# Sixteen projection pairs of a hybrid decoder block as seven-product blocks in a stage of their own

## The chip, the core and the metric

The kernel runs on one core of one Trainium2 chip. The metric is the device time of one execution, in microseconds. Before the change three runs gave 1787.57, 1789.16 and 1790.8 us (median 1789.16). The engines are called as in the profile: PE (TensorE: matmuls and transposes; PEld is its weight load, which lies beside the matmuls), DVE (VectorE), ACT (ScalarE), POOL (GpSimd) and SP (SyncE, which here issues most DMA loads). Each engine runs its own instructions strictly in the order in which they stand in the program; semaphores tie the engines together.

## The reference, cut to what matters

One decoder layer on 1024 tokens of 1024 channels. `h` is projected by one wide matrix whose columns feed two mixers and two merge gates.

```python
h = rmsnorm(x, norm_mix)
proj = h @ w_in
(rq, rk, rv, rg,                          # retention: 4 heads, dk 128, dv 256
 nq, kcr, vcr, ksl, vsl, kwn, vwn, ngate, # sparse attention: 8 heads, dk 64, 2 KV groups
 ga, gb) = split(proj)                    # merge gates, 1024 columns each
y_a = retention(rq, rk, rv, rg, ret_gn_g) @ w_ret_o
# nsa: compressed blocks (kcr, vcr through a small MLP), the top 8 of 16 selected
# blocks (ksl, vsl), a window of 512 (kwn, vwn); three softmaxes, mixed by ngate
y_b = nsa(nq, kcr, vcr, ksl, vsl, kwn, vwn, ngate, ...) @ w_nsa_o
x = x + (sigmoid(ga) * y_a + sigmoid(gb) * y_b) @ w_out
x = x + conv_ffn(rmsnorm(x, norm_ffn), ...)
return rmsnorm(x, norm_final)
```

All is float32. The kernel reaches that precision with three passes per product: an operand is split into a high and a low part (`split`: a copy on ACT that rounds to the matmul's type, then a subtraction on DVE), and `mm3` adds high x high, high x low and low x high.

## The kernel before, in words

The transposed activations `hTh`, `hTl` (high and low part, two tiles of four channel blocks each) stay in SBUF from the first stage until retention ends. The stages follow one another in the program.

1. **Norm and values** (0 to 46 us of the profiled execution). For each of 8 token tiles: load, norm (`hx`), eight transposes on PE, two splits. `values(t)`, two tiles later, multiplies a tile with the 280 columns of the values and the branch gates.
2. **Compress** (46 to 140.6 us). `proj_T` projects 128 columns of `w_in` for all 1024 tokens: 2 halves x 8 channel blocks x 3 passes = 48 matmuls of 512 columns. Called for KC and VC (by `blocks`, which builds the overlapping blocks `xr` on DVE straight out of PSUM), for the four query pairs (`queries`, to the DRAM buffer `q_scr`) and for the keys KW and KS (`keys`, into the tiles `kst`). `hidden` and `compressed` are the small MLP; its matmuls wait for `xh` and `xl`, the split blocks.
3. **Attention** (140.6 to 649.7 us). 16 units: 8 query tiles from the last to the first, 2 KV groups each; the later units see fewer keys and are shorter. A unit is a long chain across engines: scores on PE (`ps_sc`), mask and maximum on DVE (`pw`, `psl`, `pc`), exponentials on ACT, scaling on DVE, transposes on PE (`ps_pt`), split into `pth` (ACT) and `ptl` (DVE), product with the values on PE (`ps_pv`), output `ot` on DVE. Between these stand projections that have nothing to do with attention, here called the fill: after each unit `stored` projects 128 columns of a merge gate (GA, then GB) and stores them to DRAM, after every fourth unit a `ret_block` projects one head's 256 columns of retention's gate (RG), and the values (RV) of two heads close the list. A `ret_block` has 8 token tiles x 8 channel blocks x 3 passes = 192 matmuls of 256 columns.
4. **Retention** (649.7 to 870 us). Four heads. Each head projects its q and k by `proj_T`; two heads read their values from DRAM (`v_raw`), two project them in the loop over chunks.
5. **Output projections, merge, FFN** (to the end). The FFN's up projection already uses `seven`: a 2 x 2 block product in seven products instead of eight, each of 4 channel blocks x 3 passes of 512 columns, with sums and differences of the blocks (`s1` to `s4` of the activations, `t1` to `t4` of the weights).

The order of instructions on each engine is fixed when the program is built, by a scheduler that moves independent work (the fill above all) ahead into places where it reckons PE free; program order is only its starting point.

Of the kernel before, what the change touches and what calls it, by code (L numbers as in the profile page):

```python
# [10 lines left out]
F32 = mybir.dt.float32  # L11
# [7 lines left out]
P = 128  # L19
# [21 lines left out]
SPILL_V = 2  # L41
SPILL_Q = 0
# [42 lines left out]
def tile_hybrid_block(ctx: ExitStack, tc: tile.TileContext, x, norm_mix, w_in, ret_gn_g,  # L85
# [8 lines left out]

    const = ctx.enter_context(tc.tile_pool(name="const", bufs=1))
# [19 lines left out]
    rv_scr = scratch("rv_scr", SPILL_V, (S, DV))  # L115
    rq_scr = scratch("rq_scr", SPILL_Q, (P, S))
# [15 lines left out]
    def mm3(ps, ah, al, bh, bl, start, stop, more=False):  # L132
        nc.tensor.matmul(ps, ah, bh, start=start, stop=False, skip_group_check=more)  # L133
        nc.tensor.matmul(ps, ah, bl, start=False, stop=False, skip_group_check=more)  # L134
        return nc.tensor.matmul(ps, al, bh, start=False, stop=stop, skip_group_check=more)  # L135

# [54 lines left out]

    with ExitStack() as st:
        pool = st.enter_context(tc.tile_pool(name="p0", bufs=2))
        gm = pool.tile([P, D], F32, name="gm", bufs=1)
        for t in range(NT):
            xt = pool.tile([P, D], F32, name="xt", bufs=4)
            x_load = nc.sync.dma_start(xt, x[t * P:(t + 1) * P, :])
            if t == 0:
                nc.sync.dma_start(gm, bcast(norm_mix[0], D))
            if t < 3:  # L200
                value_weights(*((0, 3), (3, 3), (6, 2))[t])
# [6 lines left out]
            tok = slice(t * P, (t + 1) * P)  # L208
            for i in range(2):
# [5 lines left out]
            if t >= 2:  # L215
                values(t - 2)
        values(NT - 2)
        values(NT - 1)

    def proj_T(c0, evac, wts=None):  # L220

        wh, wl = wts or weights([(w_in, c0, P)])
        for hf in range(2):
            ps = bank("mm")
            tok = slice(hf * 512, hf * 512 + 512)
            for k in range(KD):
                mm3(ps, wh[:, k, :], wl[:, k, :], hT[k][0][:, tok], hT[k][1][:, tok],
                    k == 0, k == KD - 1)
            evac(hf, ps)

# [5 lines left out]
    with tc.issue_after(x_load.ins):  # L236
        nc.sync.dma_start(tab, tab_nsa)
# [10 lines left out]
    def blocks(c0, pos):  # L248
        c2 = [cpool.tile([P, S], F32, name=f"c2{g}") for g in range(NG)]

        def evac(hf, ps):
            t0 = hf * 512
            for g in range(NG):
                src = ps[g * DK:(g + 1) * DK, :]
                nc.scalar.activation(c2[g][0:DK, t0:t0 + 512], src, AF.Copy)
                if hf == 0:
                    nc.vector.tensor_copy(c2[g][DK:P, 0:511], src[:, 1:512])
                else:
                    nc.vector.tensor_copy(c2[g][DK:P, 511:1023], src)

        proj_T(c0, evac)
# [78 lines left out]
    def queries(pr):  # L340
        def evac(hf, ps):
            qe = npool.tile([P, 512], F32, name="ge", bufs=2)
            nc.scalar.activation(qe, ps, AF.Copy, scale=tab[:, T_QS + pr:T_QS + pr + 1])
            nc.scalar.dma_start(
                q_scr[pr][:, :, hf * 512:hf * 512 + 512].rearrange("h d t -> (h d) t"),
                qe)
        proj_T(C_NQ + pr * P, evac)


    def keys(b, c0):  # L350
        def evac(hf, ps):
            k0, k1 = (k[:, 4 * hf:4 * hf + 4, 0:P] for k in kst[b])
            ps = ps.rearrange("p (t k) -> p t k", k=P)
            nc.scalar.activation(k0[0:DK], ps[0:DK], AF.Copy)
            nc.scalar.activation(k1[DK:P], ps[DK:P], AF.Copy)
            nc.vector.tensor_sub(k0[DK:P], ps[0:DK], f32(k0[0:DK]))
            nc.vector.tensor_sub(k1[0:DK], ps[DK:P], f32(k1[DK:P]))
        proj_T(c0, evac)

    xk = blocks(C_KC, cmp_pos_k)  # L360
    xv = blocks(C_VC, cmp_pos_v)
    queries(0)
    queries(1)
    hk = hidden(xk, cmp_w1_k, cmp_b1_k, cmp_w2_k)
    hv = hidden(xv, cmp_w1_v, cmp_b1_v, cmp_w2_v)
    queries(2)
    queries(3)
# [5 lines left out]
    keys(1, C_KW)  # L373
    keys(0, C_KS)
# [154 lines left out]
    def stored(scr, c0):  # L529

        def evac(hf, ps):
            ge = npool.tile([P, 512], F32, name="ge", bufs=2)
            nc.scalar.activation(ge, ps, AF.Copy)
            nc.scalar.dma_start(scr[:, hf * 512:hf * 512 + 512], ge)
        proj_T(c0, evac)

# [24 lines left out]
    for h in range(SPILL_Q):  # L561
        stored(rq_scr[h], C_RQ + h * P)
# [3 lines left out]
    with ExitStack() as st:  # L566
# [32 lines left out]
        for h in range(H_R):  # L599
# [198 lines left out]

# [281 lines left out]
```

## Time and profile before

| | before |
|---|---|
| runs, us | 1787.57, 1789.16, 1790.8 |
| profiled execution, us | 1790.46 |
| its span, us | 1788.7 |
| PE busy | 1740.3 us, 97% |
| DVE busy | 1074.4 us, 60% |
| ACT busy | 767.5 us, 43% |
| PE instructions | 9137 |

The span is the time between the first and the last instruction of the profiled execution; 1.76 us of its time lie around it. Busy time is the union of an engine's instructions. DVE's 60% is a mean over stages of quite different load, so the stages are to be read one by one. In the windows below, the columns after the engines are the granted clock of PE (1.00 is its full speed), the mean busy share of the DMA engines and the GB/s that they moved.

### The profile page before, as it was taken

To read this page: it belongs to the slowest core of one execution; us is meant where nothing else is said; L and a number is where in the kernel's file an instruction comes from. 1 tells how busy PE (TensorE), PEld (TensorE's weight loads), DVE (VectorE), ACT (ScalarE), POOL (GpSimd) and SP (SyncE) were. 2 spreads that over 40 slices of the span, in tenths; PEclk is the share of its full clock that TensorE was granted. 3 is DMA by queue.
4 is the path that set the end of the run, shared out by engine and by line. 5 is a ranking of instruction groups with operands and counts; after the bars stand their busy time and mean duration, and the time that the engine had idled before them with its cause. 6 is when DMAs were issued, how large, how long until landed. Compare 5 with 4: busy or idle time off the path is not lost.

```text
span 1788.7 us, 24018 instructions
## 1 busy us (share of the span) xinstructions
PE 1740.3 (97%) x9137; PEld 1481.9 (83%) x9137; DVE 1074.4 (60%) x2279; ACT 767.5 (43%) x1392; POOL 87.3 (5%) x94
## 2 busy tenths in 40 slices
PE   8999999999999999999999897999999999999998
PEld 7888898988989998899778786888888888788886
DVE  6537676666766845565535337866666666644425
ACT  5435555455555644444633224443444334411102
POOL 1000000000000001221012100000000000000000
PEclk9999999999999999999999998999999999999999
DMA  6342222222221233222766411222222225723202
GB/s 208 112 143 73 68 64 62 63 74 74 62 71 57 73 115 104 78 85 77 253 206 212 165 71 59 95 79 74 94 71 94 89 77 182 230 95 94 83 1 95
DMA packets 153282, 182.52 MB, mean 102 GB/s; under 512 B 8918, under 2 KB 115918, under 8 KB 153166
## 3 DMA queue, kind: packets, MB, share of 16 engines
q1 hardware_dynamic: 124718, 138.50, 25.2%
q10 hardware_dynamic: 28448, 42.48, 6.4%
q8 instruction: 72, 1.18, 0.3%
q14 instruction: 44, 0.36, 0.1%
HBM read 134.28 MB, written 46.66 MB: 101 GB/s over the span
## 4 chain that ended last, share of the span: by engine, by line
PE 84%; DMA 7%; DVE 5%; ACT 3%; issue 1%; POOL 0%; SPq 0%; DVEq 0%; ACTq 0%; POOLq 0%
PE ps_mm L133 20%; PE ps_mm L135 20%; PE ps_mm L134 20%; PE ps_pt L509 3%; PE ps_sc L135 3%; PE ps_sc L133 3%; PE ps_sc L134 3%; PE ps_sc L396 2%; DMA sga<-ga_scr 2%; PE ps_sc L395 2%; PE ps_pv L516 2%; PE ps_pv L515 2%; PE ps_pt L134 1%; PE ps_pt L135 1%; DMA dn_raw<-in_w_down 1%; PE ps_pt L133 1%
## 5 line engine op out<-in xcount | busy, mean ns | idle before, releaser
L133 PE MATMUL ps_mm<-hTh,w_hi 128*128 128x512 f32 x512 | 203.0, 396 | 2.3 <-DVE ql L130 2.0
L134 PE MATMUL ps_mm<-hTl,w_hi 128*128 128x512 f32 x512 | 202.7, 396 | 0.0
L135 PE MATMUL ps_mm<-hTh,w_lo 128*128 128x512 f32 x512 | 202.1, 395 | 0.0
L133 PE MATMUL ps_mm<-w_hi,hTh 128*128 128x256 f32 (+1 forms) x576 | 167.0, 290 | 1.9 <-DVE kl L130 1.1
L135 PE MATMUL ps_mm<-w_hi,hTl 128*128 128x256 f32 (+1 forms) x576 | 167.2, 290 | 0.0
L134 PE MATMUL ps_mm<-w_lo,hTh 128*128 128x256 f32 (+1 forms) x576 | 166.6, 289 | 0.0
L130 DVE TENSOR_TENSOR w_lo<-w_raw,w_hi 128x1024 fp32r<-128x1024 f32 (+2 forms) x75 | 92.0, 1229 | 110.1 <-ACT w_hi L129 110.0
L1061 DVE TENSOR_TENSOR x<-ps_mm,x 128x512 f32<-128x512 f32 x96 | 66.1, 689 | 106.8 <-PE ps_mm L135 106.4
L129 ACT ACTIVATE pth<-ps_pt 128x512 fp32r<-128x512 f32 x132 | 76.6, 593 | 107.3 <-PE ps_pt L509 106.4
L133 PEld LDWEIGHTS ps_mm<-hTh,w_hi 128*128 128x128 f32 x512 | 96.8, 189 | 21.8 <-DVE ql L130 2.4
L133 PEld LDWEIGHTS ps_mm<-w_hi,hTh 128*128 128x128 f32 x576 | 110.3, 192 | 3.6 <-DVE kl L130 1.3
L130 DVE TENSOR_TENSOR ptl<-ps_pt,pth 128x512 fp32r<-128x512 f32 x132 | 89.7, 687 | 39.2 <-ACT pth L129 38.8
L129 ACT ACTIVATE w_hi<-w_raw 128x1024 fp32r<-128x1024 f32 (+2 forms) x75 | 78.4, 1047 | 80.1 <-PE ps_mm L134 50.0
L135 PEld LDWEIGHTS ps_mm<-hTh,w_lo 128*128 128x128 f32 x512 | 96.7, 189 | 18.8 <-DVE w_lo L130 0.3
L134 PEld LDWEIGHTS ps_mm<-hTl,w_hi 128*128 128x128 f32 x512 | 96.8, 189 | 18.2
L135 PEld LDWEIGHTS ps_mm<-w_hi,hTl 128*128 128x128 f32 x576 | 110.1, 191 | 1.2 <-DVE hTl L130 0.2
L134 PEld LDWEIGHTS ps_mm<-w_lo,hTh 128*128 128x128 f32 x576 | 110.2, 191 | 1.0
L133 PE MATMUL ps_mm<-wd,gd 128*128 128x512 f32 x256 | 100.4, 392 | 2.3 <-ACT gd L129 2.3
L135 PE MATMUL ps_mm<-wd,gd 128*128 128x512 f32 x256 | 100.1, 391 | 0.5 <-DVE gd L130 0.5
L134 PE MATMUL ps_mm<-wd,gd 128*128 128x512 f32 x256 | 100.0, 391 | 0.0
L395 PE MATMUL ps_sc<-kst,q 128*128 128x512 f32 (+4 forms) x216 | 70.8, 333 | 0.0
L129 ACT ACTIVATE wd<-dn_raw 128x1024 fp32r<-128x1024 f32 x16 | 16.9, 1057 | 124.2 <-PE ps_mm L135 110.3
(350 smaller groups left out, 4389.7 us busy)
## 6 DMA issues: line engine op xcount, KB each, us to landing
w_raw<-in_w_in SPq DMA_DIRECT2D x48, 512.0 KB, 3.9
wu_raw<-in_w_up SPq DMA_DIRECT2D x44, 512.0 KB, 3.5
g_scr<-rows ACTq DMA_DIRECT2D x44, 256.0 KB, 2.0
dn_raw<-in_w_down SPq DMA_DIRECT2D x22, 512.0 KB, 4.3
dn_raw<-g_scr SPq DMA_DIRECT2D x22, 512.0 KB, 4.4
xt<-in_x SPq DMA_DIRECT2D x8, 512.0 KB, 5.2
qr<-q_scr SPq DMA_DIRECT2D x64, 64.0 KB, 2.4
ga_scr<-ge ACTq DMA_DIRECT2D x16, 256.0 KB, 2.0
```

The source lines that it names most:

```text
L129: nc.scalar.activation(hi, src, AF.Copy)
L130: nc.vector.tensor_sub(lo, src, f32(hi))
L133: nc.tensor.matmul(ps, ah, bh, start=start, stop=False, skip_group_check=more)
L134: nc.tensor.matmul(ps, ah, bl, start=False, stop=False, skip_group_check=more)
L135: return nc.tensor.matmul(ps, al, bh, start=False, stop=stop, skip_group_check=more)
L395: nc.tensor.matmul(dst, q1[:, r, :], kap, start=True, stop=False)
L396: nc.tensor.matmul(dst, q2[:, r, :], kap, start=False, stop=True)
L509: nc.tensor.transpose(pt[:, r, :], pr[r][:, kt * P:(kt + 1) * P], ident)
L515: nc.tensor.matmul(pv[0:DK], v[:, 0:DK], ptl, start=False, stop=False)
L516: nc.tensor.matmul(pv, v, pth, start=False, stop=last)
L1061: nc.vector.tensor_add(x1[t][:, cs], ps, x1[t][:, cs])
```

## The change

Everything that `proj_T` did is done by `seven`, in a stage of its own between the first stage and compress. Sixteen calls of `projected(ca, cb, ...)` project two groups of 128 columns each: KC with VC, KS with KW, two of query pairs, two of RQ, two of RK, four of GA, four of GB. Rows are tokens 0-511 and 512-1023, columns the two groups, the inner dimension the two halves of the channels. Such a pair took 2 x 48 = 96 matmuls of 512 columns; as seven products it takes 7 x 12 = 84.

- The first stage visits the tokens in the order 4, 5, 6, 7, 0, 1, 2, 3 and builds the activation sums there: `f3`, `f2`, the splits `s1`, `s4`, and after the loop `s2`, `s3`.
- `pre_weights` loads 512 KB per pair and makes `t1` to `t4` and seven splits of 512 elements per row on ACT and DVE. The `last` product of one pair runs inside the next.
- All results go to DRAM (`kv_scr`, `q_scr`, `rq_scr`, `rk_scr`, `ga_scr`, `gb_scr`). `blocks` loads `c2` from `kv_scr`, `keys` loads `k_raw`, retention loads `qk_raw`.
- The pool of attention's tiles (`kst`, the table `tab`) is opened after the stage, on the memory of its sums.
- Attention's fill is the six `ret_block`s alone: the first ahead of the units, then one after units 0, 2, 4, 7 and 10. Values come from DRAM for heads 0 and 2 (before: 0 and 1).

```diff
     with ExitStack() as st:
         pool = st.enter_context(tc.tile_pool(name="p0", bufs=2))
-        for t in range(NT):
+        for n, t in enumerate(order):
...
                 split(hTh[i][:, :, tok], hTl[i][:, :, tok], pt)
-            if t >= 2:
-                values(t - 2)
...
+                if t >= 4:
+                    if i == 0:
+                        nc.scalar.activation(f3[:, :, c], pt, AF.Copy)
+                    else:
+                        nc.vector.tensor_add(f2[:, :, c], pt, f3[:, :, c])
+                        split(s1[0][:, :, c], s1[1][:, :, c], f2[:, :, c])
+                elif i == 0:
+                    nc.vector.tensor_sub(f3[:, :, c], pt, f3[:, :, c])
+                    nc.vector.tensor_sub(f2[:, :, c], f2[:, :, c], pt)
+                else:
+                    f4 = pool.tile([P, 4, P], F32, name="f4", bufs=1)
+                    nc.vector.tensor_sub(f4, pt, f2[:, :, c])
+                    split(s4[0][:, :, c], s4[1][:, :, c], f4)
...
+    with ExitStack() as st:
+        pool = st.enter_context(tc.tile_pool(name="pre", bufs=2))
...
+        def projected(ca, cb, dst, scale=(None, None)):
+            def out(i, in0, in1):
+                e = pool.tile([P, 512], F32, name="pe", bufs=3)
+                if in1 is None:
+                    nc.scalar.activation(e, in0, AF.Copy)
+                else:
+                    nc.vector.tensor_add(e, in0, in1)
...
+                nc.scalar.dma_start(dst[i % 2][:, T1 if i >= 2 else T0], e)
+
+            m = pool.tile([P, 2, 512], F32, name="m")
+            seven(blocks7, pre_weights(ca, cb), m, out)
...
+        projected(C_KC, C_VC, kv_scr[0:2])
+        projected(C_KS, C_KW, kv_scr[2:4])
...
+        for c0, n, scr in ((C_RQ, H_R, rq_scr), (C_RK, H_R, rk_scr), (C_GA, KD, ga_scr),
+                           (C_GB, KD, gb_scr)):
+            for i in range(0, n, 2):
+                projected(c0 + i * P, c0 + (i + 1) * P, scr[i:i + 2])
+        while late:
+            late.pop()()
+    sst.close()
...
-    def blocks(c0, pos):
+    def blocks(scr, pos):
         c2 = [cpool.tile([P, S], F32, name=f"c2{g}") for g in range(NG)]
...
+        for g in range(NG):
+            rows = scr[g * DK:(g + 1) * DK]
+            nc.sync.dma_start(c2[g][0:DK], rows)
+            nc.sync.dma_start(c2[g][DK:P, 0:S - 1], rows[:, 1:S])
...
+    fill = [(C_RG, rg_scr, h) for h in range(H_R)] + [(C_RV, rv_scr, h) for h in SPILL_V]
+    ret_block(*fill[0])
     for u in range(2 * NT):
         unit(NT - 1 - u // 2, u % 2)
-        scr, c0 = (ga_scr, C_GA) if u < 8 else (gb_scr, C_GB)
-        stored(scr[u % 8], c0 + (u % 8) * P)
-        if u % 4 == 3:
-            ret_block(C_RG, rg_scr, u // 4)
-    for h in range(SPILL_V):
-        ret_block(C_RV, rv_scr, h)
+        if u in (0, 2, 4, 7, 10):
+            fill.append(fill.pop(0))
+            ret_block(*fill[0])
...
-                proj_T(C_RQ + h * P, evac_q)
-            proj_T(C_RK + h * P, evac_k)
+            for scr, evac in ((rq_scr, evac_q), (rk_scr, evac_k)):
+                raw = wraw.tile([P, S], F32, name="qk_raw", tag="raw")
+                nc.sync.dma_start(raw, scr[h])
+                for hf in range(2):
+                    evac(hf, raw[:, hf * 512:hf * 512 + 512])
```

Three places show how the instructions move. The first is PE in the seventh unit of attention (unit 6; `ps_pv` takes the values' products, `ps_pt` the transposes, `ps_sc` the scores, and `ps_mm` is the fill). Before:

```order
L516 MATMUL ps_pv<-pth,vst_131 128x512
L509 MATMUL ps_pt<-ident,pw 128x128 x4
L515 MATMUL ps_pv<-ptl,vst_132 64x512
L516 MATMUL ps_pv<-pth,vst_132 128x512
L509 MATMUL ps_pt<-ident,pw 128x128 x4
L395 MATMUL ps_sc<-kst_584,q_3681 128x192
L396 MATMUL ps_sc<-kst_584,q_3682 128x192
L134 MATMUL ps_mm<-hTl_126,w_hi 128x512
L135 MATMUL ps_mm<-hTh_124,w_lo 128x512
L133 MATMUL ps_mm<-hTh_124,w_hi 128x512
L134 MATMUL ps_mm<-hTl_126,w_hi 128x512
```

The same unit now:

```order
L637 MATMUL ps_pv<-ptl,vst_145 64x512
L638 MATMUL ps_pv<-pth,vst_145 128x512
L631 MATMUL ps_pt<-ident,pw 128x128 x4
L637 MATMUL ps_pv<-ptl,vst_146 64x512
L638 MATMUL ps_pv<-pth,vst_146 128x512
L631 MATMUL ps_pt<-ident,pw 128x128 x4
L637 MATMUL ps_pv<-ptl,vst_147 64x512
L638 MATMUL ps_pv<-pth,vst_147 128x512
L631 MATMUL ps_pt<-ident,pw 128x128 x4
L637 MATMUL ps_pv<-ptl,vst_148 64x512
L638 MATMUL ps_pv<-pth,vst_148 128x512
```

The fill between the unit's steps is gone. Before, 666 matmuls of 256 columns and 344 of 512 stand between the end of unit 4 and the end of unit 15; now none does. Units 0 to 4 held 384 and 448, and 102 of 256 columns stood behind unit 15. The 960 fill matmuls that now follow the first score all stand in units 0 to 4 (275, 206, 176, 168 and 135); between the ends of units 4 and 15 DVE has 71 `ptl` and 120 scalings as before, and no `w_lo`.

The second place is PE ahead of the compress MLP, whose first matmul is `ps_sc<-w_hi,xh` (xh and xl are the split blocks that DVE and ACT make of KC). Before:

```order
L133 MATMUL ps_mm<-hTh_124,w_hi 128x512
L134 MATMUL ps_mm<-hTl_126,w_hi 128x512
L135 MATMUL ps_mm<-hTh_124,w_lo 128x512
L133 MATMUL ps_sc<-w_hi,xh 126x256
L134 MATMUL ps_sc<-w_lo,xh 126x256
L135 MATMUL ps_sc<-w_hi,xl 126x256
```

And now, where `ps_mm<-hTh,wp` is the `late` product of the last pair, GB 6 and 7:

```order
L135 MATMUL ps_mm<-hTh_138,wp 128x512
L136 MATMUL ps_mm<-hTl_140,wp 128x512
L137 MATMUL ps_mm<-hTh_138,wp 128x512
L401 MATMUL ps_pt<-ident,praw 128x16 x2
L135 MATMUL ps_sc<-w_hi,xh 126x256
L136 MATMUL ps_sc<-w_lo,xh 126x256
L137 MATMUL ps_sc<-w_hi,xl 126x256
```

Before, projections stood ahead of the MLP's first twelve matmuls and again behind them; now only two transposes of 16 columns stand between the end of the seven-product stage and the wait for `xh`, and no projection behind it until the values' MLP is through: the first `ret_block` follows it. On SP the loads of `c2` now stand behind the last weight loads of that MLP and the 990 KB table `tab`.

The third place is DVE in the first stage, two tokens' worth (`hTl` is the low part of the transposes, `f_156` is f2, `f_157` is f3, `vst` the values' low part). Before:

```order
L130 TENSOR_TENSOR hTl_125<-ps_sc,hTh_123 128x4x128
L130 TENSOR_TENSOR hTl_126<-ps_pt,hTh_124 128x4x128
L207 SCALAR_TENSOR_TENSOR hx<-xt,r,gm 128x1024
L156 TENSOR_SCALAR ms<-ss 128x1
L189 TENSOR_TENSOR vst_132<-ps_mm,vst_132 128x4x64
L190 COPY gates<-ps_mm 128x24
L207 SCALAR_TENSOR_TENSOR hx<-xt,r,gm 128x1024
L130 TENSOR_TENSOR hTl_125<-ps_sc,hTh_123 128x4x128
L130 TENSOR_TENSOR hTl_126<-ps_pt,hTh_124 128x4x128
```

And now, at the tokens where f3, f2 and s4 are built:

```order
L285 TENSOR_TENSOR f_157<-ps_sc,f_157 128x4x128
L286 TENSOR_TENSOR f_156<-f_156,ps_sc 128x4x128
L289 TENSOR_TENSOR f_382<-ps_pt,f_156 128x512
L132 TENSOR_TENSOR hTl_140<-ps_pt,hTh_138 128x4x128
L132 TENSOR_TENSOR hTl_139<-ps_sc,hTh_137 128x4x128
L285 TENSOR_TENSOR f_157<-ps_sc,f_157 128x4x128
L286 TENSOR_TENSOR f_156<-f_156,ps_sc 128x4x128
L269 SCALAR_TENSOR_TENSOR hx<-xt,r,gm 128x1024
L240 TENSOR_TENSOR vst_144<-ps_mm,vst_144 128x4x64
L241 COPY gates<-ps_mm 128x24
L132 TENSOR_TENSOR s4l<-f_382,s4h 128x4x128
```

DVE has 24 more instructions of 512 elements in this stage: two more on each of the first four tokens visited, four more on each of the others.

## Rows read from the trace of the kernel before

**Rows 1.** Windows by stage: stretch, length, busy us (xcount) PE PEld DVE ACT POOL, PEclk, DMA.

```profile
0.00:46.00 46.00, 37.18 (x266) 36.02 (x267) 31.00 (x62) 27.88 (x51) 6.30 (x14) 1.00 0.60 203
46.00:140.60 94.60, 94.15 (x470) 78.66 (x469) 44.13 (x55) 36.55 (x49) 0.00 (x0) 1.00 0.41 122
140.60:386.00 245.40, 245.40 (x1435) 211.54 (x1434) 171.01 (x522) 130.94 (x271) 10.24 (x6) 1.00 0.22 67
386.00:649.70 263.70, 263.70 (x1731) 237.00 (x1730) 184.91 (x657) 152.86 (x395) 2.52 (x2) 1.00 0.23 70
649.70:870.00 220.30, 215.26 (x1378) 194.22 (x1377) 125.88 (x301) 101.58 (x175) 37.05 (x40) 0.99 0.34 105
...
1121.00:1527.00 406.00, 405.43 (x1789) 335.83 (x1789) 271.16 (x346) 173.41 (x229) 0.00 (x0) 1.00 0.30 98
```

**Rows 2.** The chain that ended last, shares by engine, from the profile page.

```profile
PE 84%; DMA 7%; DVE 5%; ACT 3%; issue 1%; POOL 0%; SPq 0%; DVEq 0%; ACTq 0%; POOLq 0%
```

**Rows 3.** Windows, a stretch of the FFN's up products, same columns.

```profile
1150.00:1200.00 50.00, 50.00 (x222) 41.45 (x221) 33.83 (x46) 20.09 (x28) 0.00 (x0) 1.00 0.30 95
```

**Rows 4.** Timeline of PE in unit 9: start, us, instruction; first and last of eight.

```profile
560.96 0.28 PE L133 MATMUL ps_mm<-w_hi,hTh 128*128 128x256 f32 x1
...
561.79 0.28 PE L134 MATMUL ps_mm<-w_lo,hTh 128*128 128x256 f32 x1
```

**Rows 5.** Groups by line, 386 to 649.7: group xcount | busy, mean ns | idle before.

```profile
L135 PE MATMUL ps_mm<-w_hi,hTl 128*128 128x256 f32 x227 | 66.1, 291 | 0.0
L130 DVE TENSOR_TENSOR ptl<-ps_pt,pth 128x512 fp32r<-128x512 f32 x71 | 48.2, 687 | 19.1 <-ACT pth L129 18.8
...
L135 PE MATMUL ps_mm<-hTh,w_lo 128*128 128x512 f32 x114 | 45.1, 395 | 0.0
...
L130 DVE TENSOR_TENSOR w_lo<-w_raw,w_hi 128x1024 fp32r<-128x1024 f32 x14 | 17.1, 1222 | 5.8 <-ACT w_hi L129 5.8
```

**Rows 6.** Windows, units 10 to 14, columns as in rows 1.

```profile
562.00:638.00 76.00, 76.00 (x603) 72.92 (x602) 62.88 (x266) 54.21 (x168) 0.00 (x0) 1.00 0.20 59
```

**Rows 7.** Timeline of DVE: the last instructions of units 4 and 15.

```profile
385.57 0.43 DVE L525 TENSOR_TENSOR ot<-ps_pv,otmp 64x256 f32<-64x256 f32 x1
...
649.24 0.43 DVE L525 TENSOR_TENSOR ot<-ps_pv,otmp 64x256 f32<-64x256 f32 x1
```

**Rows 8.** Timeline of DVE in the first stage.

```profile
5.81 0.15 DVE L156 TENSOR_SCALAR ms<-ss 128x1 f32<-128x1 f32 x1 [4.49 <-ACT hx L204]
...
23.08 0.68 DVE L130 TENSOR_TENSOR hTl<-ps_sc,hTh 128x512 fp32r<-128x512 f32 x1
23.68 0.68 DVE L130 TENSOR_TENSOR hTl<-ps_pt,hTh 128x512 fp32r<-128x512 f32 x1
```

**Rows 9.** Timeline of PE in the FFN's norm, two tokens' transposes.

```profile
1101.28 1.94 PE L866 MATMUL ps_pt<-ident,hx 128*128 128x128 f32 x8 [5.51 <-DVE hx L826]
1108.42 1.94 PE L866 MATMUL ps_pt<-ident,hx 128*128 128x128 f32 x8 [5.20 <-DVE hx L826]
```

**Rows 10.** Chain in the compress stage: start us, us, engine tile line.

```profile
58.33 1.03 DVE xr L272
...
63.05 1.90 ACT xh L129
64.98 2.27 DVE xl L130
```

**Rows 11.** DMA issues: out<-in engine op xcount, KB each, median us to landing.

```profile
ga_scr<-ge ACTq DMA_DIRECT2D x16, 256.0 KB, 2.0
...
sga<-ga_scr SPq DMA_DIRECT2D x16, 256.0 KB, 3.9
```

**Rows 12.** Windows of low PE load, columns as in rows 1.

```profile
819.00:822.00 3.00, 1.47 (x11) 1.24 (x12) 2.94 (x4) 1.84 (x4) 0.44 (x1) 1.00 0.50 178
1101.00:1104.00 3.00, 1.94 (x8) 1.57 (x8) 2.26 (x5) 1.87 (x4) 0.00 (x0) 0.50 0.00 0
1104.00:1107.00 3.00, 0.00 (x0) 0.00 (x0) 2.52 (x7) 1.70 (x5) 0.38 (x1) 0.50 0.00 0
```

More of the change, by code (lines that the diff above doesn't have):

```diff
@@ L135, in mm3, with product, seven, kept @@
         return nc.tensor.matmul(ps, al, bh, start=False, stop=stop, skip_group_check=more)
+    def product(ps, a, b, start, stop):
+        for k in range(4):
+            mm3(ps, b[0][:, k, :], b[1][:, k, :], a[0][:, k, :], a[1][:, k, :],
+                start and k == 0, stop and k == 3, not start)
+    late = []
+    def seven(a, b, m, out):
+        a11, a12, a22, s1, s2, s3, s4 = a
+        t1, t2, t3, t4, b11, b21, b22 = b
+        def kept(ps, i):
+            nc.scalar.activation(m[:, i], ps, AF.Copy)
+            return m[:, i]
+        c = bank("sc")
+        product(c, s1, t1, True, True)
+        m5 = kept(c, 0)
+        xb = bank("mm")
+        product(xb, a11, b11, True, True)
+        m1 = kept(xb, 1)
+        while late:
+            late.pop()()
+        yb = bank("pt")
+        product(yb, a12, b21, True, True)
+        out(0, yb, m1)
+        product(xb, s2, t2, False, True)
+        u2 = kept(xb, 1)
+        product(c, s4, b22, False, True)
+        out(1, c, u2)
+        product(xb, s3, t3, False, True)
+        out(3, xb, m5)
+        def last():
+            product(xb, a22, t4, False, True)
+            out(2, xb, None)
+        late.append(last)
     def bcast(ap1d, n):
@@ L235, in tile_hybrid_block @@
     tab = npool.tile([P, T_NSA], F32, name="tab")
[L236 to L237 removed]
+    nc.sync.dma_start(tab, tab_nsa)
     kcs = [npool.tile([P, 64], F32R, name=f"kcs{g}") for g in range(NG)]
@@ L937, in up_weights @@
         split(d22[:, 0], d22[:, 1], b22)
-        return ts, [(d[:, 0], d[:, 1]) for d in (d11, d21, d22)]
+        return *ts, *((d[:, 0], d[:, 1]) for d in (d11, d21, d22))
     rows = big.tile([P, 2, 2, S], F32, name="rows", tag="A")
-    T0, T1 = slice(0, 512), slice(512, S)
-    late = []
-    def product(ps, a, b, start, stop):
-        for k in range(4):
-            mm3(ps, b[0][:, k, :], b[1][:, k, :], a[0][:, k, :], a[1][:, k, :],
-                start and k == 0, stop and k == 3, not start)
-    def seven(c0, out):
-        (t1, t2, t3, t4), (b11, b21, b22) = up_weights(c0)
-        m = fpool.tile([P, 2, 512], F32, name="m", tag="ft", bufs=4)
-        def kept(ps, i):
-            nc.scalar.activation(m[:, i], ps, AF.Copy)
-            return m[:, i]
-        c = bank("sc")
-        product(c, s1, t1, True, True)
-        m5 = kept(c, 0)
-        xb = bank("mm")
-        product(xb, a11, b11, True, True)
-        m1 = kept(xb, 1)
-        while late:
-            late.pop()()
-        yb = bank("pt")
-        product(yb, a12, b21, True, True)
-        out(0, yb, m1)
-        product(xb, s2, t2, False, True)
-        u2 = kept(xb, 1)
-        product(c, s4, b22, False, True)
-        out(1, c, u2)
-        product(xb, s3, t3, False, True)
-        out(3, xb, m5)
-        def last():
-            product(xb, a22, t4, False, True)
-            out(2, xb, None)
-        late.append(last)
     def up(f):
@@ L1017, in out_b @@
             nc.scalar.dma_start(g_scr[f + i % 2][:, tok], g)
-        seven(f * P, out_a)
-        seven(DFF + f * P, out_b)
+        for c0, out in ((f * P, out_a), (DFF + f * P, out_b)):
+            ws = up_weights(c0)
+            m = fpool.tile([P, 2, 512], F32, name="m", tag="ft", bufs=4)
+            seven((a11, a12, a22, s1, s2, s3, s4), ws, m, out)
     for f in range(0, NF, 2):
```

162 lines of the change are left out of this document (90 added, 72 removed).

## Prediction

> **What bounds the kernel now.** I read the stage windows first, then the chain, then the groups of attention's later half. PE is busy for 37 of the first 46 us, and from there on hardly ever idle: 94.15 of 94.6 us in compress, all of both halves of attention, 215.3 of 220.3 in retention [rows 1]. The chain says the same, 84% of it on PE [rows 2]. So work taken from PE is worth its time, as long as something else stands ready to fill the place. Attention needs that most. From 386.0 us (the end of unit 4) to 649.7 (the end of unit 15) [rows 7] PE is busy for 263.7 us, but much of that isn't attention: 682 matmuls of 256 columns (the row shows one of three passes) and 340 of 512 are the fill [rows 5]. A matmul of 512 columns costs 50/222 = 0.2252 us [rows 3]; eight of 256 start from 560.96 to 561.79, 0.83/7 = 0.1186 us each [rows 4]. The fill is 682 x 0.1186 + 340 x 0.2252 = 80.9 + 76.6 = 157.5 us, and attention's own PE work in these eleven units 263.7 - 157.5 = 106 us. DVE is busy there for 184.9 us, of which only the 17.1 of `w_lo` belong to the fill [rows 1, 5]: 168 us are attention's own. Without fill these units are DVE's.
>
> **What is saved.** Sixteen pairs, each 84 matmuls instead of 96: 192 x 0.2252 = 43.2 us of PE. That the new stage runs at this pace is borne out by the FFN, which uses the same function: 405.4 of 406 us busy [rows 1]. Per pair PE needs 18.9 us; DVE has 11 operations of 512 elements for the weights and 3 for the results at 0.60 us (23.08 to 23.68) [rows 8], 8.4 us, beside it. Of the stage itself I charge nothing more: PE covers it, and if the cover went the price would show as PE idle between products.
>
> **The first stage.** DVE's 31.0 us [rows 1] get 24 operations of 0.60 (14.4), four splits of 1024 elements for s2 and s3 at 1.22 (4.9; the duration of `w_lo` [rows 5]) and 11 for the first pair's weights (6.6): 56.9 us, from 5.8 us on [rows 8]. So DVE is through at 62.7 us at best. The first pair's products that wait for the last of these, three of 12 matmuls (8.1 us), and some slack put its end at 73 to 75, against 46.0 + 18.9 = 65 if nothing were late. I take +10. The low end is +4 (the scheduler lets weights and sums pass ahead of the norm). The high end comes from the nearest uncovered norm, the FFN's, where a token's transposes follow the last one's by 7.14 us [rows 9]: 5.8 + 8 x 7.14 + 6.6 + 8.1 = 78, +13; with the restart +14.
>
> **Compress.** Before, KC and VC came first, and six projections covered the making of the blocks: PE idles 0.45 us in the stage [rows 1]. Now nothing does. The loads of `c2` lie on memory that the last pair still uses, so the chain starts at the end of the stage: copy 0.6, store 2.0, load 3.9 [rows 11], then from the first `xr` to the end of `xl` 64.98 + 2.27 - 58.33 = 8.9 us [rows 10], 15.4 us in all. SP issues `c2` behind the last MLP weights and the table, which have landed or are under way; they can add a few. PE then does the keys' MLP, and the values' blocks, whose `xr`, `xh` and `xl` stand behind those of the keys on DVE and ACT, are late once more: 8.2 us of chain against the 48 matmuls of the keys' MLP. I take 5 for it, 20 in all, with 14 (the values' blocks hidden) and 28 (8 for the values, 5 for loads) as ends.
>
> **Attention.** In units 0 to 4 there is enough to do: their own PE work is 245.4 - 384 x 0.1186 - 448 x 0.2252 = 99 us [rows 1], the new fill 960 x 0.1186 = 114, 213 in all, against some 167 of DVE (171.0, with about three fewer weight splits). PE stays the bound, no idle to speak of. In units 5 to 15 no fill is left. Their length is now set by DVE's 168 us and by how well it is kept busy. At best 168. At worst as long as now, 264, if the chain of a unit (score, maximum, exponential, scale, transpose, split, product) were the limit and not the fill. The row nearest to a limit by DVE is units 10 to 14, where DVE was busy for 62.88 of 76 us, 83% [rows 6]. Some of the missing 17% was PE doing fill, which is gone, and some the wait for ACT (`ptl` for `pth`, 18.8 us of it in the eleven units [rows 5]), which stays. I take the 83%: 168/0.83 = 202 us, which leaves PE 202 - 106 = 96 us idle. The ends are 62 and 158.
>
> **Retention.** q and k leave it: 384 x 0.2252 = 86.5 us of PE, and the 102 fill matmuls that stood behind unit 15, 12.1 us. PE keeps 215.3 - 98.6 = 117 us, DVE 125.9 less eight weight splits of 1.22, 116 us [rows 1, 5]. Two engines equally loaded, working on one another's results, don't run at 100%: head 2 has no projection at all, and only heads 1 and 3 have one between the chunks. I take 15 us of new idle, with 5 and 30 (a quarter of the stage) as ends. The loads of q and k are one DMA of 512 KB each, issued ahead; I cost them at nothing, since unit 15 and the head before cover them, and at their landing time of about 4 us per head without that cover, inside the 30.
>
> **The sum** against the profiled execution, 1790.5: - 43.2 + 10 + 20 + 96 + 15 = +97.8, so 1888 us. That execution is 1.3 us above the median of the runs, which is less than I can tell here. The change takes 43 us from an engine, and takes the work that kept this engine busy out of the stage that had no other.
>
> **The rivals.**
>
> 1. *DVE packs fully.* With PE at once at hand for every transpose and score, the eleven units last 168 us. For it: DVE's waits for PE were waits behind fill. Against it: a unit's instructions follow one another across four engines. The idle is 62 instead of 96: 1854 us.
>
> 2. *PE's clock falls in units 5 to 15.* PE would be busy for about half of this time, in short pieces. The trace shows both answers. From 819 to 822 us PE is busy 1.47 of 3 us and the granted clock stays 1.00 (2.4 GHz); from 1101 to 1107, after a stretch without matmuls, it is 0.50 (1.2 GHz) with 1.94 and 0.00 us of work in 3 [rows 12]. At half the clock attention's own 106 us become 212, PE is the bound again, and at the same 83% the units last 255 us. The idle of 96 becomes 149: 1941 us. With the clock down for half of the time it is some 1915. The Trainium skill, page "TensorE: Matmul & The Clock Gate", section "A second HAM failure mode: psum-queue depth-cycling", describes a kernel in which short idles between groups of matmuls, while PSUM banks are cycled, made the clock swing between its two levels, so that single matmuls looked as fast as ever and throughput fell. That is how units 5 to 15 would look, and it speaks against this change; by that rule the sum would be nearer to 1941 than to 1888. The window at 819 us doesn't bear it out, that at 1101 us does, but is far emptier.
>
> 3. *The other side: no slower.* For this, all new idle together must stay under 43 us. The mechanism would have to be in attention, in units 5 to 15: DVE's instructions there would have to run faster once PE no longer reads and writes PSUM beside them. With the other three terms at their low ends (4 + 14 + 5 = 23) the units may last 106 + 20 = 126 us, so DVE's 168 would have to shrink by a quarter; from there on the change is no loss. Against it: `ptl` takes 687 ns [rows 5] where fill is dense and `hTl` of the same shape 0.68 in the first stage [rows 8], where PE does much less. With a shrink of 30%, 118 us, the sum is 1790.5 - 43 + 23 + 12 = 1782.
>
> 4. *The seven products don't save what they should.* If the results' path (ACT's copies, DVE's sums, four stores per pair) held PE up by 2 us per pair, 32 us come on top: 1920. The FFN's stage speaks against it.
>
> **How the numbers follow.** My forecast, 1888, gets 0.53, with a range of its own of 1865 to 1912 (the three smaller terms at their ends together, half of the time). Full packing gets 0.14, the clock 0.22 (0.08 of it above 1950, where a slow start and a slow retention join it), rival 4 gets 0.05, the other side 0.06. For 8 in 10 I leave out the other side, the lower part of full packing and the upper part of the clock case: 1845 to 1950. A difference of 0.2%, 3.6 us, is about what a measurement of this kernel can tell from none (the three runs spread over 3.2). Faster by more than that gets 0.04, within it 0.02, slower 0.94, all but the rival of the other side.
>
> **What would show it.** In the profile after: PE's work 43 us smaller, and its idle time, 48 us now, near 190. The seven-product stage of about 303 us (1344 x 0.2252) with PE at 99% or more. One gap of about 15 us at the end of it and a smaller one in the MLP. In the eleven later units, PE near 106 us of work and DVE near 168 in some 200 us, with the clock at 1.00; a clock of 0.50 and longer matmuls there would be rival 2, DVE above 95% rival 1. I am wrong if these units stay as full as they were, or if DVE's work in them is far from 168 us.

## The result and the profile after

The changed kernel takes 1907.28 us (median of four runs, 1902.25 to 1910.42) against 1789.98 for the kernel before in the same series: ratio 1.0655, 95% interval 1.0629 to 1.0681. Slower by 117 us; forecast were 98 more, 1888, with a range of 1845 to 1950.

The page of the profile after, its span, busy times and chain (those of before are in the table and in [rows 2]):

```profile
span 1905.8 us, 24152 instructions
PE 1762.0 (92%) x8945; PEld 1485.8 (78%) x8945; DVE 1188.3 (62%) x2487; ACT 816.7 (43%) x1500; POOL 86.8 (5%) x94
...
PE 75%; DVE 11%; DMA 7%; ACT 4%; issue 2%; SPq 0%; POOL 0%; DVEq 0%; POOLq 0%; ACTq 0%
```

PE's share of the chain has fallen from 84% to 75%, DVE's risen from 5% to 11%. PE is busy 22 us longer than before although it has 43 us less to do; the last section says where its matmuls took longer. The windows of the changed kernel, cut at the first and the last product of the new stage, the first score, the ends of units 4 and 15 and the first matmul of retention's output projection (columns as in [rows 1]):

```profile
0.00:46.73 46.73, 34.96 (x246) 33.10 (x247) 38.25 (x72) 29.81 (x55) 5.42 (x14) 1.00 0.49 160
46.73:362.63 315.90, 309.54 (x1356) 255.38 (x1354) 158.92 (x241) 111.60 (x194) 0.00 (x0) 0.99 0.34 112
362.63:432.08 69.45, 43.27 (x313) 41.81 (x313) 33.33 (x43) 25.92 (x33) 0.00 (x0) 0.78 0.56 158
432.08:644.44 212.36, 211.26 (x1565) 197.40 (x1563) 161.37 (x519) 120.04 (x257) 10.15 (x6) 1.00 0.18 56
644.44:820.91 176.47, 141.72 (x709) 106.17 (x709) 161.09 (x634) 120.44 (x352) 2.69 (x2) 0.88 0.08 21
820.91:1008.63 187.72, 153.91 (x964) 139.47 (x965) 126.74 (x303) 100.93 (x172) 36.87 (x40) 0.83 0.48 153
```

Behind that last cut the two kernels run alike: 1905.8 - 1008.6 = 897.2 us now, 1788.7 - 892.3 = 896.4 before. Retention, from the end of unit 15 to there, took 242.7 before:

```profile
649.67:892.33 242.66, 234.84 (x1456) 208.45 (x1455) 135.40 (x309) 112.48 (x190) 37.05 (x40) 0.99 0.39 120
```

What each stage lost can be worked out as its length less PE's work at full pace, with the paces of [rows 3, 4]:

| | work of PE | length | lost | lost before | forecast, new loss | measured, new loss |
|---|---|---|---|---|---|---|
| first stage and new stage | 37.2 + 1344 x 0.2252 = 339.9 | 362.6 | 22.7 | 8.8 | 10 | 13.9 |
| compress, up to the first score | MLP 94.15 - 360 x 0.2252 = 13.1, first block 22.8 | 69.5 | 33.6 | 0.5 | 20 | 33 |
| units 0 to 4 | 213 | 212.4 | 0 | 0 | 0 | 0 |
| units 5 to 15 | 106 | 176.5 | 70 | 0 | 96 | 70 |
| retention | 234.8 - 98.6 = 136.2 | 187.7 | 51.5 | 7.8 | 15 | 43.7 |

(360: of the 384 projection matmuls of the old stage, 24 stand behind the first score in the order.) The new losses less the saving of 43.2 make 117. The sum came out 19 us above the forecast: retention (29 us), compress (13) and the start (4) were forecast too small, units 5 to 15 (26) too large. That errors of 46 and 26 us in opposite directions leave 19 is in part luck.

### The profile page after: what moved, and what is told of

The parts are those of the page before. It is cut to its first block, busy times and chain, and to the rows that moved or that the text cites. A ratio compares the mean times of both kernels' runs of the same rounds, so it can differ in the third digit from the quotient of the medians.

```text
span 1905.8 us, 24152 instructions
## 1 busy us (share of the span) xinstructions
PE 1762.0 (92%) x8945; PEld 1485.8 (78%) x8945; DVE 1188.3 (62%) x2487; ACT 816.7 (43%) x1500; POOL 86.8 (5%) x94
## 4 chain that ended last, share of the span: by engine, by line
PE 75%; DVE 11%; DMA 7%; ACT 4%; issue 2%; SPq 0%; POOL 0%; DVEq 0%; POOLq 0%; ACTq 0%
PE ps_mm L135 16%; PE ps_mm L136 16%; PE ps_mm L137 16%; PE ps_sc L136 4%; PE ps_sc L135 4%; PE ps_sc L137 4%; PE ps_pt L631 2%; PE ps_pt L135 2%; PE ps_pt L136 2%; PE ps_pt L137 2%; PE ps_sc L518 1%; PE ps_pv L637 1%; PE ps_sc L517 1%; PE ps_pv L638 1%; DVE ptl L132 1%
## 5 line engine op out<-in xcount | busy, mean ns | idle before, releaser
L162 ACT ACTIVATE m<-ps_mm 128x512 f32<-128x512 f32 x76 | 45.4, 598 | 98.6 <-PE ps_mm L137 83.2
L132 DVE TENSOR_TENSOR w_lo<-w_raw,w_hi 128x1024 fp32r<-128x1024 f32 (+2 forms) x43 | 51.6, 1201 | 56.4 <-ACT w_hi L131 54.4
L517 PE MATMUL ps_sc<-kst,q 128*128 128x512 f32 (+4 forms) x216 | 78.6, 369 | 3.3 <-DVE nmax L532 2.3
L131 ACT ACTIVATE wp<-t 128x512 fp32r<-128x512 f32 x64 | 40.1, 628 | 92.2 <-PE ps_mm L137 63.5
L637 PE MATMUL ps_pv<-ptl,vst 128*64 128x512 f32 x132 | 59.3, 449 | 18.5 <-DVE ptl L132 17.6
L518 PE MATMUL ps_sc<-kst,q 128*128 128x512 f32 (+4 forms) x216 | 72.0, 340 | 0.0
L131 ACT ACTIVATE d<-wu_raw 128x512 fp32r<-128x512 f32 x66 | 39.6, 626 | 65.3 <-DMA wu_raw<-in_w_up 50.1
L131 ACT ACTIVATE w_hi<-w_raw 128x1024 fp32r<-128x1024 f32 (+2 forms) x43 | 44.6, 1039 | 47.9 <-DMA w_raw<-in_w_in 13.5
L132 DVE TENSOR_TENSOR d<-wu_raw,d 128x512 fp32r<-128x512 f32 x66 | 44.6, 688 | 32.2 <-ACT d L131 32.2
```

The costliest lines, as they stand in the source:

```text
L131: nc.scalar.activation(hi, src, AF.Copy)
L132: nc.vector.tensor_sub(lo, src, f32(hi))
L162: nc.scalar.activation(m[:, i], ps, AF.Copy)
L517: nc.tensor.matmul(dst, q1[:, r, :], kap, start=True, stop=False)
L518: nc.tensor.matmul(dst, q2[:, r, :], kap, start=False, stop=True)
L637: nc.tensor.matmul(pv[0:DK], v[:, 0:DK], ptl, start=False, stop=False)
```

## Experiments

All are edits of the changed kernel. The kernel before gave 1786 to 1792 us in the different series, so differences of a few us between series are read from the stages in the traces, not from the times.

**1. Does DVE set the pace of units 5 to 15?** Their clock had fallen to 0.88 in the mean, so PE at half speed was the other candidate. The trace after has both: eight stretches of 20 us,

```profile
684.00:704.00 20.00, 16.21 (x91) 12.06 (x90) 19.62 (x71) 14.87 (x36) 0.11 (x1) 1.00 0.07 20
...
724.00:744.00 20.00, 17.25 (x77) 12.81 (x76) 17.16 (x62) 13.22 (x39) 0.00 (x0) 0.74 0.07 20
...
784.00:804.00 20.00, 17.23 (x85) 14.09 (x83) 19.54 (x98) 14.17 (x52) 0.00 (x0) 0.74 0.07 20
```

show the clock at 1.00 in some and 0.74 in others, while DVE is busy for 17.2 to 19.6 of 20 us in all eight. The first edit takes work of DVE away and leaves PE's; it leaves out the low part of the probabilities:

```diff
...
-                split(pth, ptl, pt)
+                if qi < 6 and (qi, g) != (5, 0):
+                    nc.scalar.activation(pth, pt, AF.Copy)
+                    ptl = pth
+                else:
+                    split(pth, ptl, pt)
```

> From unit 5 on the low part ptl of the probabilities is left out (the product with it reads pth again, so its result is not the reference's): 71 DVE operations of 512 elements at 0.60 us, 43 us, go from units 5 to 15; ACT, PE and the order of the fill stay. Theory (DVE sets the pace there, busy for 161 of 176 us, and PE's clock of 0.88 costs little): these units take 135 to 150 us, 1867 to 1881 us. Rival (PE sets it, at the lowered clock, busy for 142 of 176): 168 to 176 us, 1899 to 1907.

Measured: 1867.08 us (ratio to before 1.0449, 1.0427 to 1.0471). The eleven units, in the window of this run:

```profile
646.44:784.70 138.26, 121.25 (x707) 93.34 (x706) 121.13 (x563) 116.86 (x352) 2.69 (x2) 0.98 0.09 27
```

138.3 us instead of 176.5: 38 us less, and DVE is busy for 40 less (43 were expected). And the clock is 0.98 with the same PE instructions in less time, so that PE is busy for 121 us instead of 142. DVE sets the pace; the low clock comes with the slack that DVE leaves PE. The edit also makes the chain of each step shorter, so alone it doesn't tell DVE's load from the length of that chain. DVE's 161 busy of 176.5 us do: any other cause has at most 15 us.

**2. Is PE's idle time there free?** If so, more fill costs nothing (three blocks computed a second time), and fill that comes back from the stage pays (GB projected between the units again).

```diff
+        if u in (5, 7, 9):
+            ret_block(C_RG, rg_scr, (u - 5) // 2)
```

> Three blocks of retention's gate are computed a second time (576 more matmuls of 256 columns, 68.3 us of PE, emitted after units 5, 7 and 9); nothing is taken away. Theory (DVE sets the pace of units 5 to 15, PE's 70 us idle there are free): plus 0 to 15 us, 1907 to 1922. Rival (PE at a lowered clock sets it): plus 68, 1975 us. If the clock falls for want of work and the fall is what the units pay for, the added work brings the clock back and costs nothing or less than nothing, 1900 to 1907.

```diff
-        ... (C_GA, KD, ga_scr), (C_GB, KD, gb_scr)):
+        ... (C_GA, KD, ga_scr)):
...
+        if 3 <= u < 11:
+            stored(gb_scr[u - 3], C_GB + (u - 3) * P)
```

> Merge gate GB goes back to attention: eight projections of 384 matmuls of 512 columns in all (86.5 us of PE) after units 3 to 10, and its four pairs (4 x 84 x 0.2252 = 75.7 us) leave the stage. Theory (PE's idle time in units 5 to 15, 176.5 - 106 = 70 us, is free because DVE sets the pace there): the fill costs 16 to 25 us instead of 86, so 1907 - 75.7 + 16 to 25, 1848 to 1857 us. Rival (these units are set by PE at a lowered clock, so that fill costs its full time): 1907 - 76 + 86 = 1918 us.

Measured: 1936.84 us (ratio 1.0828, 1.0805 to 1.0850) and 1887.52 (1.0556, 1.0536 to 1.0577). Neither theory nor rival: 68.3 us of fill cost 30, 86.5 us cost 56 (the stage is 76.8 us shorter, the time only 20). The units 5 to 15 of the two, in the same order:

```profile
647.06:851.11 204.05, 186.33 (x1253) 161.95 (x1251) 166.14 (x644) 130.22 (x366) 2.52 (x2) 0.96 0.13 39
```

```profile
582.05:798.68 216.63, 196.22 (x1176) 163.65 (x1174) 168.25 (x645) 132.40 (x368) 2.53 (x2) 0.96 0.13 40
```

PE is busy for 91% of the time in both, DVE for 81% and 78%. The fill isn't spread over the slack: the scheduler puts it into the next units in order, which PE then bounds, and the last units stay as dry as they were. In the first run all fill stands in units 0 to 9, in the second in units 0 to 8, and PE is busy for 100% of units 0 to 8 and 0 to 7.

**3. Would the same fill cost less if it were spread?** Chunks of 48 matmuls may not start before given `ps_pv` matmuls of given units (the tiles, stores and weights stay).

```diff
+                marks.append(nc.tensor.matmul(pv, v, pth, start=False, stop=last))
...
+                    at = marks[(slot[0] * 16 + n) * len(marks) // (slot[1] * 16)] if marks else None
+                    with tc.issue_after(at.ins) if at else ExitStack():
                         mm3(ps[:, j, :], ...)
...
+        slot[1] = (2, 2, 2, 2, 1, 1, 1, 1, 1, 1, 1, 1, 1, 1, 1, 1)[u]
```

> The same fill, but its chunks of 48 matmuls may not start before given instructions of given units: two chunks behind each of units 0 to 3, one behind each of the others. Theory (the scheduler spends all fill in units 0 to 4, which PE then bounds at 212 us, and leaves units 5 to 15 to DVE at 176 us; over all 16 units PE has 319 us of work and DVE 322): spread out, attention takes 355 to 365 us instead of 389, and 9 us of fill pass into retention; 1873 to 1885 us. Rival (each unit's own chain over four engines sets its time and the chunks delay it wherever they stand): 1900 to 1915.

Measured: 1892.38 us (ratio 1.0559, 1.0542 to 1.0576), between theory and rival. Attention takes 373.5 us instead of 388.8: units 0 to 4 get 37 us shorter, units 5 to 15 21 us longer.

```profile
430.90:606.50 175.60, 162.43 (x1037) 138.28 (x1035) 152.12 (x512) 109.08 (x241) 10.15 (x6) 0.97 0.14 43
606.50:804.37 197.87, 177.69 (x1225) 158.82 (x1226) 167.36 (x641) 129.56 (x366) 2.53 (x2) 0.97 0.13 39
```

So where the fill stands matters: the loss falls from 70 to 56 us. The rest stays: with PE at 90% DVE falls from 91% to 85% in the later units, and its waits grow, those for `pth` from 2.8 to 8.2 us and those for `ps_sc` from 6.2 to 9.0. That these steps wait behind a running chunk is likely from the order on PE, but no run shows it apart.

**4. The gap behind the new stage.** Two edits: the first `ret_block` is written ahead of `blocks`; and `c2`, `praw` and `posT` get memory that the stage doesn't use.

> The first ret_block is written ahead of the compress blocks, nothing else changes. Theory (the 32.7 us lost between the last product and the first score are PE with nothing to do while KC and VC come back from DRAM): 155 of its matmuls, 18.4 us, now stand in the gap, 14 to 20 us less, 1887 to 1893 us. Rival (the gap is SP's queue; the block's two weight loads stand ahead of the loads of c2 and push them back as far): no change, 1907 us.

```diff
+    epool = est.enter_context(tc.tile_pool(name="early", bufs=1, side="right"))
...
-        c2 = [cpool.tile([P, S], F32, name=f"c2{g}") for g in range(NG)]
+        c2 = [epool.tile([P, S], F32, name=f"c2{g}") for g in range(NG)]
```

> The tiles c2, praw and posT of compress get memory of their own (8.6 KB per partition, taken from the second buffer of m and the third of pe in the stage), so that KC is loaded back during the stage and not after the last pair's stores. Theory (most of the 32.7 us lost between the last product and the first score come from the reuse of memory; leaving the sums out took 20 us from there): the 18.3 us from the last product to the first matmul on xh become 8 to 10, 1896 to 1899 us; xl and the values' blocks are late as before. Rival (the gap is the chain of DVE and ACT from c2 to xl): under 3 us, 1904 to 1907.

Measured: 1897.83 us (ratio 1.0618, 1.0594 to 1.0642) and 1895.84 (1.0617, 1.0598 to 1.0636). The chain of the changed kernel says what the gap is made of (start us, us, what):

```profile
363.28 2.85 DMA gb_scr<-pe
366.14 0.52 SPq L396
...
369.71 5.04 DMA w2r<-in_cmp_w_k
374.75 0.26 PE ps_pt L401
...
380.16 3.88 DMA w2r<-in_cmp_w_v
...
388.51 1.90 ACT xh L131
...
395.42 5.45 DMA b1b<-in_cmp_b_v
```

The last pair's store ends at 366.1, and only then does SP issue the loads of `c2`, `praw` and the rest, of which the last lands at 374.8. Two more loads follow on the chain later, `w2r` for the values and `b1b`. With `c2` apart the wait of 12.1 us for these loads is gone, and PE's two longest waits are for the making of the blocks and for the MLP's `hl`:

```profile
PE ps_sc L135 <- ACT xh L131: 8.9, 1, 8.9
PE ps_sc L136 <- DVE hl L132: 2.9, 1, 2.9
```

The stretch from the last product to the first score shrinks from 69.5 to 58.8 us, as the theory had it. The early block does fill the gap, with less gain than the theory had: the first score comes 4.9 us sooner although 81 more fill matmuls (9.6 us) lie ahead of it. But these 9.6 us are then missing between the units, and attention's loss grows from 70 to about 74. Filling one hole from a fixed stock opens another.

**5. What the activation sums cost.**

```diff
-        blocks7 += [s1, s2, s3, s4]
+        blocks7 += [(hTh[i][:, :, h], hTl[i][:, :, h])
+                    for i, h in ((0, T1), (0, T0), (1, T0), (1, T1))]
```

> The activation sums f2, f3, s1 to s4 are left out and the seven products read plain blocks of h in their place (the projections are then not those of the reference); every product, weight sum and store stays. Theory (DVE's 28 more operations in the first stage delay the first pair): of the 22.7 us that PE loses up to the last product, 8.8 are the old start; 10 to 14 less, 1893 to 1897 us. Rival (the delay is the first pair's weights or the new order of the tokens): 1903 to 1907.

Measured: 1880.93 us (ratio 1.0506, 1.0485 to 1.0527), a larger gain than the theory's. The end of the last product comes 8.0 us sooner (354.7), not 10 to 14: two fifths of the start's 13.9 aren't the sums. The other 20 us are a find: without the sums' 64 KB per partition, compress no longer waits for memory, its blocks `xr` are built during the stage (343.9 to 354.7 us), and the stretch up to the first score is 48.95 us instead of 69.45.

```profile
354.68:403.63 48.95, 40.78 (x311) 39.08 (x310) 24.29 (x36) 23.19 (x30) 0.00 (x0) 0.92 0.59 180
```

Of the 33 us newly lost there about 20 are thus memory, handed from the stage to compress.

**6. Do the seven products save what they should?** The same stage with eight products per pair.

```diff
+            for i in range(4):
+                ps = bank("mm")
+                h = T1 if i >= 2 else T0
+                for k in range(KD):
+                    wh, wl = b[k // 4][i % 2]
+                    mm3(ps, wh[:, k % 4, :], wl[:, k % 4, :], hT[k][0][:, h], hT[k][1][:, h], ...)
+                out(i, ps, None)
```

> The stage stays, but each pair is done with eight block products, 96 matmuls, instead of seven, and without the weight sums. Theory (the seven products do save what they should, 192 x 0.2252 = 43.2 us, and the loss is all elsewhere): plus 43, less up to 10 at the start, where a plain product needs no sums: 1940 to 1950 us. Rival (the way of the seven products' results through ACT, DVE and the stores costs PE part of the saving): 1915 to 1935.

Measured: 1943.29 us (ratio 1.0852, 1.0834 to 1.0870), 36 above the changed kernel.

```profile
47.56:398.77 351.21, 350.19 (x1550) 289.69 (x1548) 53.83 (x79) 87.25 (x145) 0.00 (x0) 1.00 0.31 100
```

The stage takes 351.2 us for 1536 matmuls, 345.9 at full pace; with seven products it took 315.9 for 302.7. The saving of 43 us is real, and 8 us of it are lost again at the stage's start, where the plain products needn't wait for sums.

**7. Retention.** Its q and k are projected there again and the four pairs leave the stage.

```diff
-        for c0, n, scr in ((C_RQ, H_R, rq_scr), (C_RK, H_R, rk_scr), (C_GA, KD, ga_scr),
+        for c0, n, scr in ((C_GA, KD, ga_scr),
...
-            for scr, evac in ((rq_scr, evac_q), (rk_scr, evac_k)):
-                ...
+            proj_T(C_RQ + h * P, evac_q)
+            proj_T(C_RK + h * P, evac_k)
```

> Retention projects its q and k itself again (384 matmuls of 512 columns, 86.5 us), and the four pairs RQ and RK (75.7 us) leave the stage. Theory (from the end of attention to the first output projection 44 us are lost because PE has too little beside the chains of DVE and ACT, and its clock falls): the work fills that, 1907 - 75.7 + 86.5 - 30 to 44 = 1874 to 1888 us. Rival (the loss is the start of retention and the loads from DRAM, which stay): 1907 + 11 = 1918 us.

Measured: 1867.72 us (ratio 1.0445, 1.0415 to 1.0475). That is a larger gain than the theory's. Of the 384 matmuls 336 stand in retention, and the scheduler moves 48 ahead into attention. Retention takes 217.8 us, 30 more than in the changed kernel, and attention 7.6 more: of the 86.5 us some 49 were free.

```profile
752.21:970.05 217.84, 210.36 (x1308) 187.38 (x1309) 129.51 (x306) 108.03 (x183) 36.70 (x40) 0.98 0.39 124
```

The chain of the changed kernel shows what they cover (pieces of retention's first two heads):

```profile
820.94 1.82 DMA o_scr<-ot
823.93 0.43 SPq L747
824.41 7.17 DMA sg<-rg_scr
...
837.66 3.58 DMA w_raw<-in_w_in
...
872.39 3.66 DMA v_raw<-rv_scr
...
878.58 3.87 DMA v_raw<-rv_scr
```

Retention's own tiles lie on attention's memory: ACT's first split of q waits 3.0 us for the store of the last `ot`, and SP issues the loads of the gate `sg` (7.2 us) only behind that store. The raw q and k of the first head don't wait: they lie in the buffers of the weights and were loaded at 518 and 555 us. Later the weights (3.6 us) and `v_raw` stand on the chain. PE's three longest waits of this stage in the changed kernel, in sum, and a window at its start:

```profile
PE ps_mm L135 <- ACT w_hi L131: 7.8, 2, 6.4
PE ps_pt L843 <- ACT rets L836: 7.4, 7, 2.2
PE ps_pt L135 <- DVE kkl L132: 6.8, 1, 6.8
```

```profile
820.40:847.40 27.00, 15.78 (x67) 14.71 (x68) 19.91 (x39) 14.48 (x22) 6.75 (x5) 0.50 0.49 163
```

The wait for `kkl` is the start on attention's memory (the last `ot`, its store, then the splits of q and k), `rets` are the normalized results of the chunks, and the longest wait for `w_hi` is for weights of the attention's output projection. With the projections back PE is idle for 7.5 us in this stage instead of 33.8, and the clock is 0.98 instead of 0.83. How much of the loss is loads, how much the chains of DVE and ACT and how much the clock, no run separates.

**8. Together.** Three of the edits (q and k back, first block early, spread), then also GB back and `c2` apart.

> Three of the edits together: retention projects q and k itself, the first block stands ahead of compress, the other fill is spread over the units. If the three losses are separate places, their gains add: 39.5 + 9.5 + 24 to 34 from 1907, 1824 to 1834 us. If they share one cause (PE short of work wherever DVE is busy), the sum is smaller: 1840 to 1858.

> All in one: retention projects q and k itself, GB is projected between the units again (one half-gate of 96 matmuls after every second unit), the first block stands ahead of compress, the other blocks are spread, and KC is loaded back early. The stage keeps eight pairs (saving 96 matmuls, 21.6 us). Theory (the place of the work, not the seven products, is what costs): 1849 less 5 to 10 for KC and 20 to 35 for GB, 1804 to 1824 us, still above the kernel before by what the start (8 us) and the rest of the gaps cost. If the gap behind the stage is already filled by the first block, KC gives nothing and the time is 1814 to 1829.

Measured: 1849.01 us (ratio 1.0328, 1.0307 to 1.0348) and 1827.41 (1.0232, 1.0214 to 1.0251). The first three gains add to 39.6 + 9.5 + 14.9 = 64; together they gave 58, so they are nearly separate places, and the expected sum was too hopeful chiefly by the spreading. The last version took 22 us more off, in the range given for the case that KC gives nothing. (A projection of GB has 48 matmuls, not 96; eight of them make 384.) With half of the pairs in the stage and the three gaps treated, it is still 41 us above the kernel before: of the 21.6 us that its eight pairs save nothing is left. Worked out as in the table, it newly loses 34 us in attention, 22 in compress and 11 up to the last product, and gets 9 back in retention. Its attention alone, 433 us, holds 414 of PE busy time; in the kernel before it is the full 509 of 509. No version here beats the kernel before. Seven products as fill between the units, where the plain projections stood, are an open rival that no run tests.

## Why the prediction was right, and where its terms were not

*The direction and the mechanism.* Right. The fill ends with unit 4, units 0 to 4 are bound by PE (212.4 us, forecast 213), units 5 to 15 by DVE; experiment 1 shows the latter, and DVE's work there is 161 us, forecast 168. Two of its signs did not come: the clock of 1.00 in these units (0.88), and PE's idle time near 190 us. That is 144 (1905.8 - 1762.0), since 65 us of the loss stand as matmuls that took longer. And the total is closer than its terms: compress and retention lie above their own upper ends of 28 and 30 us, and units 5 to 15 made up for most of it.

*Units 5 to 15: 96 us idle forecast, 70 lost.* The step that took the 83% of units 10 to 14 was too low: DVE is busy for 91%. Before, half of DVE's idle time in these units (79 us) were waits for PE behind fill, which I had named and not taken off: 40 us for `ps_sc` and `ps_pt`, now 8. The longest of before, then of now:

```profile
DVE ptl L130 <- ACT pth L129: 18.8, 19, 3.9
DVE pw L410 <- PE ps_sc L396: 12.5, 11, 2.0
DVE pw L410 <- PE ps_pt L509: 9.4, 6, 3.8
```

```profile
DVE pw L532 <- PE ps_sc L518: 4.4, 8, 0.9
DVE ptl L132 <- ACT pth L131: 2.8, 4, 1.7
DVE psl L532 <- PE ps_sc L518: 1.8, 4, 0.8
...
DVE pw L532 <- PE ps_pt L631: 1.4, 2, 0.8
```

The wait for `pth`, which the prediction said would stay, fell from 18.8 to 2.8 us: it went with the fill, and `pth` itself waits for PE's transposes. Rival 1 (62 us idle) lay nearer here, but not its total.

*Compress: 20 forecast, 33 measured.* The chain after the store was costed right as a mechanism, with loads of 3.9 us, and 4 us short. In fact six issues stand one behind the other on SP (366.1 to 369.7), and the loads behind them land together at 374.8; from the end of the store to the first `xr` 9 us went by, not 4. The values' blocks, which I gave 5 us, cost PE 1.8. Left out of the sum were two waits of PE later in the MLP, 2.9 us for `hl` (behind the load of `b1b`, 5.4 us) and 2.1 for the first block's weights, and 7 us of matmuls that took longer, at a clock of 0.78 (43.3 us busy for 35.9 of work).

*Retention: 15 forecast, 44 measured.* The term that failed most. The new 44 us are 26 of PE idle (33.8 against 7.8) and 18 of matmuls that took longer (153.9 us busy for 136.2 of work). What was put at nothing, the loads of q and k "since unit 15 and the head before cover them", did cost little: ACT waited 2.1 us for them. The step that failed is the 15 us for two engines working on one another's results. It left out that retention starts on attention's memory (6.8 us of PE until the first splits are through), that the other loads, of the gate, the values and the weights, come to stand on the chain, and the clock. What hid all this before was the projection of q and k, the very work that leaves (experiment 7). I named head 2 as the one without a projection; head 0, with which the stage begins, is another.

*Start: 10 forecast, 13.9 measured*, within its bounds; the sums are 8 of it.

*Rival 2, the clock.* Half right: it does fall, for short stretches, and to the level named (1.2 GHz):

```profile
732.00:741.50 9.50, 8.44 (x30) 6.33 (x29) 7.24 (x26) 3.06 (x6) 0.00 (x0) 0.50 0.08 22
```

But it costs little in these units: DVE is idle for 15 us there, and no more than that can be the clock's. Experiment 1 brought the clock back by taking work from DVE. What it costs in compress and retention, no run shows apart. The section "A second HAM failure mode: psum-queue depth-cycling" of the Trainium skill's page "TensorE: Matmul & The Clock Gate" describes another kernel, in which short idles between matmul groups made the clock swing between its levels; the trace agrees (0.74 to 1.00 in stretches of 20 us, with 22 waits of PE for `ptl`, 2.2 us at most). That this costs throughput, which the section reports of that kernel, this case doesn't show for units 5 to 15.

*Rivals 3 and 4* fell: DVE's operations kept their length (`ptl` 683 ns in units 5 to 15, 687 before), and experiment 6 found the saving.

## What to carry to other kernels

Count what work is for before moving it: a projection that stands between the steps of a stage bound by another engine, or in front of loads that can't start earlier, is paid for by that stage, and here saving an eighth of it didn't buy the cover back. Before gathering such work in a stage of its own, add up each later stage's two engines without it. And ask whose memory the next stage's first loads land on; some 20 us of compress and part of the first 7 us of retention were waits for tiles to be given back.

## What the runs showed that was not expected

The same PE instructions of units 5 to 15 ran at a granted clock of 0.88 when they took 176.5 us and of 0.98 when they took 138.3. In the changed kernel PE's busy time over all is 1762 us for about 1697 us of work at full pace (1740.3 - 43.2). These 65 us are matmuls that took longer: 36 us in units 5 to 15, 18 in retention, 7 in compress. They are not the clock alone. In experiment 1 PE is busy for 121 us at a clock of 0.98 with the same 106 us of work: a matmul's record is longer (395 ns for 512 columns [rows 5]) than its step in a dense stream (0.2252 us), and one that stands alone counts in full. So a rise of PE's busy time doesn't show a fall of its clock.

Two engines that feed one another were never both full in these eleven units: DVE 91% with PE's work at 60%, 85% and 81% with PE busy at 90% and 91%, 70% with PE at 100% [rows 1].
